# Two-block transformer on one core: the experts' part as a fixed chain of steps, with 21 weight places

## The chip, the core and the metric

The program runs on one core of a Trainium2 chip. TensorE (PE) multiplies matrices into PSUM, VectorE (DVE) and ScalarE (ACT) work element by element, GpSimd (POOL) does small side work, and SyncE (SP) issues the transfers of weights from device memory (HBM) to the on-chip memory. The metric is the device time of one execution in microseconds (us); less is better.

## What is computed

x has 256 tokens of 1024 features. A first block of two layers runs mixed attention (compressed, selected and windowed attention, gated linear attention, spatial gating) and a gated FFN of width 2816. A second block of one layer runs dilated and sliding-window attention and then a mixture of experts:

```python
g_top = argmax(hf @ w_group + b_group)            # one of 4 groups per token
ids   = 2 best of the 8 experts of that group      # weights e_w, scaled by the group's probability
for e in range(32):
    a = silu(hf @ w_e_gate[e]) * (hf @ w_e_up[e])  # 1024 -> 512
    out = out + gates[:, e:e+1] * (a @ w_e_down[e])
return rmsnorm_2(x + out, g_final)
```

hf is the normed x. All 32 experts' weights are read in fp32: three matrices of 2 MB each.

## The kernel before

All instructions of the listing are recorded through one helper, so nearly every row of the profile has its line, L257; tiles tell the parts apart. `raw`, `raw_right` and `raw_left` are places for weights, 2048 fp32 columns on 128 partitions (1 MB) each; `arena` is the main arena for temporaries, `arena_y` that of the second block's attention; `y_hi` and `y_lo` hold its outputs, `h_hi` and `h_lo` the normed input in two parts for products in fp32r, `whi` and `wlo` the same for weights.

**Weights.** `Stream` holds a list of units in the order of use. `pump` issues the next units on SP's queue into the free places, in that order, and `free` gives a place back after its last matmul. A place that was lent by the arena goes back to the arena after one use. A dense unit is split on ACT and DVE into hi and lo; experts' units are used as fp32. A pair of experts q (of 16) has 12 units: eight for gate and up (two row halves, two experts, two matrices) and four for down. The order is rows and down of each pair, except that at the end it is rows 14, rows 15, down 14, down 15. Places: seven `raw` throughout; five `raw_right` once the attention's outputs are used up in `mix2`; three `raw_left` once the output projection has finished; and three of the arena, lent once, at the start of `route`. That is 18.

**Routing.** `t_xg` transposes x, weighs it with the norm's gain and computes the logits; `route` finds group, experts and, with a triangular matmul, each token's place among the at most 32 rows (`CAP`) of an expert. `h_rows` scales x by gain and norm and splits it into `h_hi` and `h_lo`.

**Experts.** They run in four batches of eight. `t_batch` builds the one-hot matrix (token to row), gathers the rows by matmuls with it into `xe` in four steps k2 of eight products, and builds `gt`, the gated matrix for the way back, from 24 small DVE operations and eight transposes. It is a task beside the main line: `S.tick` and `S.until` let a planner with its own clock emit its steps between those of the main line. A pair's rows are 32 matmuls of 32 rows by 512 columns, four at a time on different column strips of TensorE; each fp32 matmul leaves two records in the trace. `t_act` (tanh, two DVE products, four transposes, a copy) is such a task too, and the down product of pair q-1 stands between the two row halves of pair q:

```python
if h == 0 and 1 <= q < NQ - 1:
    self.emit_down(q - 1)
```

Two pairs fill `Y`, which `emit_scatter` adds to the tokens in PSUM banks 0 to 3. `last_norm` closes with the norm and the stores. A branch (L2315) handles experts with more than 32 rows.

Of the kernel before, what the change touches and what calls it, by code (L numbers as in the profile page):

```python
# [6 lines left out]
F32 = mybir.dt.float32  # L7
# [43 lines left out]
LENT = 3  # L51
# [518 lines left out]
class Kernel:  # L570
# [992 lines left out]
    def plan2(self):  # L1563
# [31 lines left out]

        for q in range(NQ):
# [255 lines left out]
    def mix2(self):  # L1852
# [57 lines left out]
    def t_xg(self, c):  # L1910
# [6 lines left out]
        s = slice(c * 512, c * 512 + 512)  # L1917
# [22 lines left out]
        if c == 0:  # L1940
            self.xgr = yield from self.ar.new(2, D)
        else:
            self.norm_rstd(self.rstd)
        (nc.vector if c else nc.gpsimd).tensor_tensor(
            out=self.xgr[:, :, s],
            in0=self.x[:, :, s],
            in1=self.gffn[:, s].unsqueeze(1).to_broadcast([P, 2, 512]),
            op=ALU.mult,
        )

    def route(self):
# [36 lines left out]
        for tb in range(2):  # L1988
            self.h_rows(tb)
        self.ar.drop(self.xgr, self.gffn)  # L1990
# [67 lines left out]
    def overflow(self):  # L2058
# [3 lines left out]
        new = self.ar.try_new  # L2062
        ov = new((2, NE))

        w = [t.rearrange("p (k c) -> p k c", k=4) for t in self.st.slots[:2]]
        assert self.st.issued == len(self.st.units) and len(w) == 2
        xg = new((NK, T))
        a, th, at = new((2, 512)), new((512,)), new((4, T))
# [7 lines left out]
        two = (self.ps(4), self.ps(6))  # L2076
# [37 lines left out]
        self.emit_x()  # L2114
        self.ar.drop(ov, xg, a, th, at)

    def h_rows(self, tb):

        nc = self.nc
        hi = self.h_hi.rearrange("p a b -> p (a b)")[:, tb * D : tb * D + D]  # L2120
        lo = self.h_lo.rearrange("p a b -> p (a b)")[:, tb * D : tb * D + D]
        t, r = self.xgr[:, tb], self.rstd[:, tb : tb + 1]
        if tb:
            nc.scalar.activation(out=t, in_=t, func=AF.Copy, scale=r)
        else:
            nc.gpsimd.tensor_scalar(out=t, in0=t, scalar1=r, scalar2=1.0, op0=ALU.mult, op1=ALU.mult)
        nc.scalar.copy(out=hi, in_=t)
        nc.gpsimd.tensor_tensor(out=lo, in0=t, in1=hi.bitcast(F32), op=ALU.subtract)

    def t_batch(self, b):  # L2130


        nc, S = self.nc, self.side
        d = self.onehot[:, b % 2]
        e0 = b * 8
        for tb in range(2):
            nc.vector.tensor_tensor(
                out=d[:, tb].rearrange("p (e s) -> p e s", e=8),
                in0=self.place[:, tb, e0 : e0 + 8].unsqueeze(2).to_broadcast([P, 8, CAP]),
                in1=self.tab("iota").unsqueeze(1).to_broadcast([P, 8, CAP]),  # L2140
                op=ALU.is_equal,
            )
        xe = self.xe[b] = yield from self.ar.new(NK, 8 * CAP)
        hi = self.h_hi.rearrange("p a b -> p (a b)")
        lo = self.h_lo.rearrange("p a b -> p (a b)")
        for k2 in range(4):

            bk = [k2] if b == 0 else (yield from S.get(1))
            ps = self.ps(bk[0])
            for i in range(2):  # L2150
                k = k2 * 2 + i
                n = 0
                for tb in range(2):

                    c0 = tb * D + (k // 4) * 512
                    c = slice(c0 + k % 4, c0 + 512, 4)
                    for h in (hi, lo):
                        self.mm(ps[:, i * 256 : i * 256 + 256], h[:, c], d[:, tb, :], n == 0, n == 3)
                        n += 1
            if b:  # L2160
                yield
            self.evict(xe[:, k2 * 2 : k2 * 2 + 2, :].rearrange("p a b -> p (a b)"), ps)
            if b:
                S.put(bk)
            S.done.add(("xe", b, k2))
            yield
        if b == 0:
            self.gates()
        dg = yield from self.ar.new(2, 2, 3, 2 * CAP)
        for tb in range(2):  # L2170
            for pr in range(2):
                for i in range(6):
                    e = e0 + 4 * pr + i % 4
                    nc.vector.tensor_scalar(
                        out=dg[:, tb, pr, i // 2, i % 2 * CAP : i % 2 * CAP + CAP],
# [463 lines left out]
```

## Time and profile before

| | us |
|---|---|
| median of 3 runs | 1471.01 |
| lowest, highest | 1468.20, 1473.86 |
| the profiled execution | 1472.58 |
| its span in the trace | 1470.8 |
| busy in it: PE, DVE, ACT, POOL | 1294.8, 740.4, 558.8, 226.4 |
| DMA traffic | 360.75 MB, mean 245 GB/s |

The profile is of one execution. Busy shares are averages over very different stages: the two layers and the second attention take the first two thirds, the experts the last. There TensorE is reported busy for much of the time, but its records are stretched by a low clock, so the GB/s row and the waits say more than the busy row.

### The profile page before, as it was taken

What the parts mean: (1) busy time and instruction counts of PE and PEld (TensorE: products, weight loads), DVE (VectorE), ACT (ScalarE), POOL (GpSimd) and SP (SyncE); (2) the same over time, 40 slices, a digit from 0 to 9 for tenths busy, and PEclk for the clock granted to TensorE, in tenths of its full rate; (3) what the DMA queues carried; (4) which work ended last, traced back from release to release, by engine and by line L of the source; (5) the groups of instructions that cost most, each with busy time, mean ns of one, the idle gap of its engine ahead of it and who ended that gap; (6) DMA issues with size and microseconds to landing.
All of it is one profiled execution on the core that took longest, in us unless ns stands there. A gap on an engine that the chain in (4) does not pass through costs nothing. (4 is left out here: it accounts for less than half of the span.)

```text
span 1470.8 us, 22896 instructions
## 1 busy us (share of the span) xinstructions
PE 1294.8 (88%) x8791; PEld 966.9 (66%) x8791; DVE 740.4 (50%) x1573; ACT 558.8 (38%) x1167; POOL 226.4 (15%) x348
## 2 busy tenths in 40 slices
PE   8989999999999999999999999978876857776576
PEld 8767999988777899988889999853323212311111
DVE  5587778756587677755766564663021200201001
ACT  5535655555526555555555455431000100100001
POOL 2154111101154111123332210120000000000000
PEclk9999999999999999999999999988987778787778
DMA  9551565556452566566435353697999899899995
GB/s 340 190 184 45 174 200 173 186 159 218 138 168 68 159 186 189 184 193 194 140 116 172 115 173 120 214 379 298 420 421 420 363 420 420 352 420 420 420 417 242
DMA packets 153558, 360.75 MB, mean 245 GB/s; under 512 B 8640, under 2 KB 98240, under 8 KB 128736
## 3 DMA queue, kind: packets, MB, share of 16 engines
q1 hardware_dynamic: 151328, 354.81, 66.1%
q0 software_dynamic: 1328, 3.63, 0.8%
q8 instruction: 71, 1.16, 0.3%
q10 hardware_dynamic: 784, 0.76, 0.2%
q14 instruction: 47, 0.39, 0.1%
HBM read 358.12 MB, written 1.05 MB: 244 GB/s over the span
## 5 line engine op out<-in xcount | busy, mean ns | idle before, releaser
L257 DVE TENSOR_TENSOR wlo<-raw,whi 128x512 fp32r<-128x512 f32 (+3 forms) x560 | 404.9, 730 | 255.4 <-ACT whi L257 243.2
L257 ACT CAST whi<-raw 128x512 fp32r<-128x512 f32 (+3 forms) x560 | 337.7, 606 | 341.6 <-PE psum L257 271.6
L257 PE MATMUL psum<-h_hi,whi 128*128 128x256 f32 x1040 | 296.0, 285 | 3.0 <-ACT whi L257 3.0
L257 PE MATMUL psum<-h_lo,whi 128*128 128x256 f32 x1040 | 290.6, 279 | 0.1
L257 PE MATMUL psum<-h_hi,wlo 128*128 128x256 f32 x1040 | 290.6, 279 | 0.2 <-DVE wlo L257 0.2
L257 PE MATMUL psum<-raw,arena 128*32 128x512 f32 x704 | 181.7, 696 | 58.9 <-DMA raw<-in_w_e_gate_dram 47.5
L257 DVE COPY arena<-psum 128x384 f32<-128x384 f32 (+4 forms) x68 | 38.1, 560 | 346.9 <-ACT arena L257 232.7
L257 PEld LDWEIGHTS psum<-h_hi,whi 128*128 128x128 f32 x1040 | 195.8, 188 | 10.1 <-issue 4.8
L257 PEld LDWEIGHTS psum<-h_lo,whi 128*128 128x128 f32 x1040 | 195.9, 188 | 0.9 <-issue 0.5
L257 PEld LDWEIGHTS psum<-h_hi,wlo 128*128 128x128 f32 x1040 | 195.8, 188 | 0.4 <-DVE wlo L257 0.4
L257 PE MATMUL psum<-raw_right,arena 128*32 128x512 f32 x496 | 143.8, 671 | 24.7 <-DMA raw_right<-in_w_e_gate_dram 17.1
L257 PE MATMUL psum<-whi,h_hi 128*128 128x256 f32 (+3 forms) x448 | 145.7, 325 | 1.4 <-ACT arena_o L257 1.1
L257 PE MATMUL psum<-whi,h_lo 128*128 128x256 f32 (+3 forms) x448 | 138.2, 308 | 0.0
L257 PE MATMUL psum<-wlo,h_hi 128*128 128x256 f32 (+3 forms) x448 | 138.1, 308 | 0.0
L257 PEld LDWEIGHTS psum<-raw,arena 128*32 128x32 f32 x704 | 38.8, 122 | 148.7 <-DMA raw<-in_w_e_gate_dram 62.5
L257 PE MATMUL psum<-raw_left,arena 128*32 128x512 f32 x312 | 110.3, 714 | 26.3 <-DMA raw_left<-in_w_e_gate_dram 20.4
L257 PE MATMUL psum<-arena 64*128 64x256 f32 (+10 forms) x668 | 115.4, 381 | 6.7 <-DVE arena L257 4.7
L257 ACT COPY arena<-psum 128x384 f32<-128x384 f32 (+3 forms) x61 | 32.0, 524 | 221.8 <-PE psum L257 212.4
L257 ACT ACTIVATE arena<-psum 128x256 f32<-128x256 f32 (+3 forms) x38 | 18.1, 476 | 240.7 <-PE psum L257 228.6
L257 POOL TENSOR_TENSOR arena<-arena 128x512 f32<-128x512 f32 (+2 forms) x46 | 49.2, 1079 | 295.6 <-DVE arena L257 286.6
L257 PEld LDWEIGHTS psum<-whi,h_hi 128*128 128x128 f32 x448 | 85.0, 190 | 11.0 <-issue 4.4
L257 PEld LDWEIGHTS psum<-arena 64*128 64x128 f32 (+4 forms) x668 | 63.0, 178 | 42.2 <-issue 22.1
(240 smaller groups left out, 1823.9 us busy)
## 6 DMA issues: line engine op xcount, KB each, us to landing
raw<-in_w_in_dram SPq DMA_DIRECT2D x60, 512.0 KB, 4.9
raw<-in_w_e_up_dram SPq DMA_DIRECT2D x30, 1024.0 KB, 19.8
raw<-in_w_e_down_dram SPq DMA_DIRECT2D x30, 1024.0 KB, 19.9
raw<-in_w_e_gate_dram SPq DMA_DIRECT2D x28, 1024.0 KB, 19.9
raw<-in_w_gate_dram SPq DMA_DIRECT2D x44, 512.0 KB, 4.0
raw<-in_w_up_dram SPq DMA_DIRECT2D x44, 512.0 KB, 5.0
raw_right<-in_w_e_down_dram SPq DMA_DIRECT2D x22, 1024.0 KB, 19.9
raw<-in_w_down_dram SPq DMA_DIRECT2D x20, 1024.0 KB, 5.1
```

The source lines that it names most:

```text
L257: return f(*args, **kw)
```

## The change

- The one-hot gather takes x itself in fp32 (`h_rows`, `xgr` and the 0.5 MB load of the norm's gain go). The gain is applied when the product is copied to `xe`, per feature from the small tile `gp`; the norm's factor is applied per expert row in the activation (`scales`, `rhe`, `r2e`).
- `t_batch` becomes `side_batch`, a list of eight steps: `places`, four `rows`, `scales`, two `back`. `back` builds a half of the gated matrix with four DVE operations. `moe` takes the steps from a list at fixed points, one or two at a time; the planner is not asked any more.
- A pair is one chain: rows half 0, steps, rows half 1, activation with steps, transposes, down of the same pair. The order of units is rows and down for each pair, and the last down is in eight units of 0.5 MB, column half 0 ahead of half 1, each followed by its scatter, squares and product with the final gain.
- Five fp32 matmuls without use (`WARM`) stand at the start of `route`.
- Places: seven `raw`; two in `arena_y` from the end of the attention on; three `raw_right`; one kept for good in the main arena, two lent once beside it, one more lent when `mx` is done; five `raw_left`, over the space of `h_hi`, `h_lo`, `whi` and `wlo`. That is 21. The one-hot matrix also lies in `arena_y`. The main arena is 96 columns smaller.

```diff
-LENT = 3
+WARM = 5
+LENT = 2
@@ plan2
         for q in range(NQ):
             rows(q)
-            if q < NQ - 2:
-                down(q)
-        down(NQ - 2)
-        down(NQ - 1)
+            (down if q < NQ - 1 else last_down)(q)
@@ mix2
         self.open_raw("right")
-        self.gffn = self.ar.now(D)
-        nc.gpsimd.dma_start(out=self.gffn, in_=self.A["g_ffn_2"].to_broadcast([P, D]))
+        self.st.slots.append(self.room(2048))
+        self.lend(LENT)
...
                 S.until(("mx", k))
+                if c == 0 and k == NK - 1:
+                    self.ar.drop(mx)
+                    self.lend(1)
                 self.dense_T(acc, self.h_hi, self.h_lo, [k], start=k == 0, stop=k == NK - 1)
-            if c == 1:
-                self.ar.drop(mx)
-                self.open_raw("left")
@@ route
         S.until(("xg", 0), ("xg", 1))
-        S.free = [7]
-        for _ in range(LENT):
-            self.st.lend(self.ar.now(2048), self.ar.drop)
-        self.st.pump()
+
+        self.open_raw("left")
+        self.ar.drop(self.xg)
+        for _ in range(WARM):
+            self.mm(self.ps(0), self.ident, self.x[:, 0, 0:512], True, True)
...
-        for tb in range(2):
-            self.h_rows(tb)
-        self.ar.drop(self.xgr, self.gffn)
@@ new functions
+    def lend(self, n):
+
+        for _ in range(n):
+            self.st.lend(self.room(2048), self.ar.drop)
+        self.st.pump()
...
+        def rows(k2):
+            xe = self.xe[b]
+
+            ps = self.ps(7 if b else k2).rearrange("p (k c) -> p k c", k=2)
             for i in range(2):
                 k = k2 * 2 + i
                 for tb in range(2):
 
+                    c0 = (k // 4) * 512
+                    self.mm(ps[:, i, :], self.x[:, tb, c0 + k % 4 : c0 + 512 : 4], d[:, tb, :], tb == 0, tb == 1)
+            gain = lambda k: self.gp[:, k // 4, k % 4 : k % 4 + 1]
+            k = k2 * 2
+            nc.scalar.activation(out=xe[:, k, :], in_=ps[:, 0, :], func=AF.Copy, scale=gain(k))
+            nc.vector.tensor_scalar(out=xe[:, k + 1, :], in0=ps[:, 1, :], scalar1=gain(k + 1), scalar2=None, op0=ALU.mult)
...
+        steps = [places] + [lambda k2=k2: rows(k2) for k2 in range(4)] + [scales]
+        return steps, [lambda pr=pr: back(pr) for pr in range(2)]
@@ moe
+            self.emit_rows(q, 0)
+            if q == 1:
+                todo += late
...
+            side(2)
+            self.emit_rows(q, 1)
+            if q == 0:
+                side(1)
+            th = self.emit_act(q)
+            side(2)
             if q % 4 == 3:
+                side(99)
                 self.ar.drop(self.xe.pop(b))
+            at = self.emit_at(th)
+            side(1)
             if q == NQ - 1:
...
+                break
+            self.emit_down(q, at, None)
+            self.ar.drop(at)
+            if q % 2:
+                todo[:0] = [lambda quad=q // 2, c=c: self.emit_scatter(quad, c) for c in range(2)]
+            side(1)
+        self.last_norm(at)
@@ last_norm
         for c in range(2):
+            self.emit_down(NQ - 1, at, c)
+            self.emit_scatter(NQ // 2 - 1, c)
             for tb in range(2):
@@ open_raw
         if side == "right":
-            self.ar.shrink("b")
             self.close("right")
-            n = 45 // 8
+            n = 3
         else:
             self.close("split")
-            n = 3
+            self.close("h")
+            n = 5
@@ body
+        self.ar.shrink("b")
+        self.st.slots += [self.arena_y[:, i * 2048 : i * 2048 + 2048] for i in range(2)]
+        self.onehot = self.arena_y[:, 4096 : 4096 + 32 * CAP].rearrange("p (b t c) -> p b t c", b=2, t=2)
+        self.st.pump()
         self.mix2()
```

Three places show how the order of instructions changes (the helper has line L258 in the changed kernel). The first is SP's queue at the opening of the last places, each row one unit of 1 MB. Before:

```order
L257 DMA raw5_86<-in_w_e_down_2_dram 128x2048
L257 DMA raw_left0_9339<-in_w_e_gate_2_dram 128x2048
L257 DMA raw_left1_9340<-in_w_e_up_2_dram 128x2048
L257 DMA raw_left2_9341<-in_w_e_gate_2_dram 128x2048
L257 DMA arena_88<-in_w_e_up_2_dram 128x2048
L257 DMA arena_88<-in_w_e_gate_2_dram 128x2048
L257 DMA arena_88<-in_w_e_up_2_dram 128x2048
L257 DMA raw2_83<-in_w_e_gate_2_dram 128x2048
```

In the changed kernel:

```order
L258 DMA arena_86<-in_w_e_down_2_dram 128x2048 x3
L258 DMA raw3_82<-in_w_e_gate_2_dram 128x2048
L258 DMA arena_y_6387<-in_w_e_up_2_dram 128x2048
L258 DMA arena_86<-in_w_e_gate_2_dram 128x2048
L258 DMA arena_y_6387<-in_w_e_up_2_dram 128x2048
L258 DMA raw_left0_9375<-in_w_e_gate_2_dram 128x2048
L258 DMA raw_left1_9376<-in_w_e_up_2_dram 128x2048
L258 DMA raw_left2_9377<-in_w_e_gate_2_dram 128x2048
L258 DMA raw_left3_9378<-in_w_e_up_2_dram 128x2048
L258 DMA raw_left4_9379<-in_w_e_down_2_dram 128x2048
L258 DMA raw4_83<-in_w_e_down_2_dram 128x2048
```

Before, `raw_left` and after it the three arena units end the list of 18, and the last row goes to the first place that a pair has to free. Now the units in the arena and in `arena_y` come ahead of `raw_left`, whose five end the list of 21; the last row is again the first that a pair has to free.

The second is TensorE's queue from the last transposes of x to the first expert product; `s` is the one-hot selection that the ranking matmul reads. Before:

```order
L257 MATMUL psum<-tab_67,x 128x128 x8
L257 MATMUL psum<-wr,arena 128x36 x8
L257 MATMUL psum<-s_9417,tab_67 128x64
L257 MATMUL psum<-s_9417,ones 128x32
L257 MATMUL psum<-onehot,h_hi 128x256
L257 MATMUL psum<-onehot,h_lo 128x256
```

In the changed kernel:

```order
L258 MATMUL psum<-tab_67,x 128x128 x8
L258 MATMUL psum<-wr,arena 128x36 x8
L258 MATMUL psum<-x,tab_67 128x512 x5
L258 MATMUL psum<-s_9426,tab_67 128x64
L258 MATMUL psum<-s_9426,ones 128x32
L258 MATMUL psum<-arena_y,x 128x256 x8
L258 MATMUL psum<-raw_83,arena 32x512
L258 MATMUL psum<-raw_81,arena 32x512
L258 MATMUL psum<-raw_84,arena 32x512
L258 MATMUL psum<-raw_79,arena 32x512
```

Five products of x with the identity now stand ahead of the ranking matmul, and the gather reads x and `arena_y` (the one-hot matrix) in fp32 in one piece of two steps.

The third is VectorE's queue behind the branch for overfull experts, to the end of the program. Before:

```order
L257 SCALAR_TENSOR_TENSOR arena<-arena,psum 64x512
L257 TENSOR_TENSOR arena<-arena,psum 64x512
L257 COPY arena<-psum 64x512 x2
L257 TENSOR_TENSOR arena<-psum,arena 128x512 x4
L257 TENSOR_SCALAR arena<-arena,rstd 128x512 x2
```

In the changed kernel:

```order
L258 SCALAR_TENSOR_TENSOR arena<-arena,psum 64x512
L258 SCALAR_TENSOR_TENSOR arena<-arena,r2e,psum 64x512
L258 TENSOR_TENSOR arena<-psum,arena 128x512 x2
L258 COPY arena<-psum 64x512
L258 TENSOR_TENSOR arena<-psum,arena 128x512 x2
L258 TENSOR_SCALAR arena<-arena,rstd 128x512 x3
```

The two copies of `Y` and the four products with the final gain stood in two blocks; now a pair of products stands behind the work on column half 0 and ahead of the copy for half 1, and VectorE scales three of the four last tiles.

## Rows read from the trace of the kernel before

**Rows 1.** The page's forty slices of 36.8 us: granted clock and GB/s.

```profile
PEclk9999999999999999999999999988987778787778
...
GB/s 340 190 184 45 174 200 173 186 159 218 138 168 68 159 186 189 184 193 194 140 116 172 115 173 120 214 379 298 420 421 420 363 420 420 352 420 420 420 417 242
```

**Rows 2.** Stretches: from:to, length, granted clock, DMA share, GB/s.

```profile
980.00:994.00 14.00, 0.54 1.01 425
994.00:1005.00 11.00, 0.81 0.10 20
...
1005.00:1100.00 95.00, 0.87 1.01 419
...
1140.00:1155.00 15.00, 0.61 0.72 279
...
1265.00:1285.00 20.00, 0.67 0.74 294
```

**Rows 3.** SP's issues in order of time: start us, duration, queue, destination<-source.

```profile
951.14 0.33 SPq L257 DMA_DIRECT2D raw_right<-in_w_e_gate_dram  x1
...
977.79 0.33 SPq L257 DMA_DIRECT2D raw_left<-in_w_e_gate_dram  x1
...
980.34 0.42 SPq L257 DMA_DIRECT2D arena<-in_w_e_up_dram  x1
1003.38 0.33 SPq L257 DMA_DIRECT2D raw<-in_w_e_gate_dram  x1
```

**Rows 4.** SP's waits from 1005 on (us, times, longest); a page row of issues.

```profile
SPq L257 <- PE psum L257: 135.3, 36, 19.5
SPq L257 <- DMA raw<-in_w_e_up_dram: 41.0, 20, 3.8
...
raw<-in_w_e_up_dram SPq DMA_DIRECT2D x30, 1024.0 KB, 19.8
```

**Rows 5.** Timeline of the routing: start us, duration, engine, operation, count [idle before].

```profile
979.87 2.48 PE L257 MATMUL psum<-wr,arena 128*128 128x36 f32 x16 [0.35 <-DVE arena L257]
...
984.02 4.65 POOL L257 TENSOR_TENSOR h_lo<-arena,h_hi 128x1024 fp32r<-128x1024 f32 x2 [1.16 <-ACT h_hi L257]
...
984.66 1.74 DVE L257 TENSOR_TENSOR tt<-el,top8a 128x16 f32<-128x16 f32 x1
...
986.43 2.26 DVE L257 TENSOR_TENSOR tt<-tt,tab 128x16 f32<-128x16 f32 x1
...
989.55 0.17 DVE L257 TENSOR_TENSOR tt<-e,top8b 128x16 f32<-128x16 f32 x1
...
990.88 0.69 PE L257 MATMUL psum<-s,tab 128*128 128x64 f32 x2 [8.53 <-DVE s L257]
```

**Rows 6.** Timeline of the first pair on TensorE.

```profile
999.37 0.51 PE L257 MATMUL psum<-onehot,h_hi 128*128 128x256 f32 x1
...
1001.45 1.92 PE L257 MATMUL psum<-raw,arena 128*32 128x512 f32 x16
```

**Rows 7.** Timeline of the work for batch 2 of the experts, three rows.

```profile
1137.69 5.04 DVE L257 TENSOR_SCALAR arena<-tab,place,g 128x32 f32<-128x32 f32 x24
...
1143.65 0.59 ACT L257 ACTIVATE arena<-psum 64x512 f32<-64x512 f32 x1 [0.99 <-PE psum L257]
...
1147.20 3.64 PE L257 MATMUL psum<-raw_right,arena 128*32 128x512 f32 x16 [0.47 <-ACT arena L257]
```

**Rows 8.** Timeline of the end.

```profile
1435.26 1.06 PE L257 MATMUL psum<-raw_right,arena 128*32 128x512 f32 x1 [2.29 <-DMA raw_right<-in_w_e_up_dram]
...
1440.53 0.59 ACT L257 ACTIVATE arena<-psum 64x512 f32<-64x512 f32 x1 [9.70 <-PE psum L257]
...
1458.36 0.58 ACT L257 COPY arena<-psum 64x512 f32<-64x512 f32 x1 [9.56 <-PE psum L257]
...
1458.99 3.70 PE L257 MATMUL psum<-arena 128*128 128x512 f32 x8 [0.68 <-ACT arena L257]
...
1463.57 0.18 POOL L257 TENSOR_TENSOR v<-ssq 128x2 f32<-128x2 f32 x1 [136.00 <-ACT psum L257]
```

More of the change, by code (lines that the diff above doesn't have):

```diff
@@ L1939, in t_xg @@
                 yield
-        if c == 0:
-            self.xgr = yield from self.ar.new(2, D)
-        else:
+        if c:
             self.norm_rstd(self.rstd)
[L1944 to L1949, printed above, removed]
     def route(self):
@@ L2135, in t_batch @@
         e0 = b * 8
[L2136 to L2145, printed above, removed]
@@ L2146, in t_batch, with places @@
-        for k2 in range(4):
-            bk = [k2] if b == 0 else (yield from S.get(1))
-            ps = self.ps(bk[0])
+        def places():
+            for tb in range(2):
+                nc.vector.tensor_tensor(
+                    out=d[:, tb].rearrange("p (e s) -> p e s", e=8),
+                    in0=self.place[:, tb, e0 : e0 + 8].unsqueeze(2).to_broadcast([P, 8, CAP]),
+                    in1=self.tab("iota").unsqueeze(1).to_broadcast([P, 8, CAP]),
+                    op=ALU.is_equal,
+                )
+            self.xe[b] = self.room(NK, 8 * CAP)
@@ L2160, in t_batch @@
[L2160 to L2175, printed above, removed]
-                        in0=self.tab("iota"),
-                        scalar1=self.place[:, tb, e : e + 1],
-                        scalar2=self.gate[:, tb, e : e + 1],
-                        op0=ALU.is_equal,
-                        op1=ALU.mult,
-                    )
-            yield
@@ L2183, in t_batch @@
-        gt = yield from self.ar.new(2, 2, T)
-        for pr in range(2):
-            bk = yield from S.get(1)
-            ps = self.ps(bk[0])
+                    c0 = (k // 4) * 512
[4 more added lines that the diff above has]
+            nc.vector.tensor_scalar(out=xe[:, k + 1, :], in0=ps[:, 1, :], scalar1=gain(k + 1), scalar2=None, op0=ALU.mult)
@@ new lines, in scales @@
+        def scales():
+            ps = self.ps(7)[0:64, 0:4]
+            for q in range(4):
+                for tb in range(2):
+                    self.mm(ps[:, q : q + 1], d[:, tb, q * 64 : q * 64 + 64], self.rstd[:, tb : tb + 1], tb == 0, tb == 1)
+            rh, r2 = self.small([64, 4], "rhe", bufs=2), self.small([64, 4], "r2e", bufs=2)
+            nc.scalar.activation(out=rh, in_=ps, func=AF.Copy, scale=0.5)
+            nc.vector.tensor_tensor(out=r2, in0=rh, in1=rh, op=ALU.mult)
+            self.re[b] = rh, r2
@@ L2206, in t_act, with emit_act @@
+    def emit_act(self, q):
+        nc = self.nc
+        gu = self.ps(4)
+        rh, r2 = (t[:, q % 4 : q % 4 + 1] for t in self.re[q // 4])
+        th = self.room(512)
+        nc.scalar.activation(out=th[0:64], in_=gu[0:64], func=AF.Tanh, scale=rh)
         nc.vector.scalar_tensor_tensor(
@@ L2257, in emit_scatter @@
[L2257 to L2272 removed]
+                    self.st.free(units[(c or 0) * 4 + k // 2 * 2 + x])
@@ L2274, in moe @@
+        if not odd:
+            self.Y = self.room(2, 512)
+        for i in cs:
+            copy = nc.scalar.copy if i == 0 else nc.vector.tensor_copy
+            copy(out=self.Y[r[i] : r[i] + 64, i], in_=y[r[i] : r[i] + 64])
     def moe(self):
-        nc, S = self.nc, self.side
+        nc = self.nc
         self.gates = self.route()
-        self.xe, self.gt, self.at = {}, {}, {}
+        self.xe, self.gt, self.re = {}, {}, {}
         nb = NQ // 4
-        S.start(self.t_batch(0), ("batch", 0))
```

300 lines of the change are left out of this document (145 added, 155 removed).

## The prediction

> **What bounds the kernel now.** I read the page's forty slices first, then a table of stretches, then the DMA issues, the waits of the issuing queue and the end. The slices [rows 1] split the span in two. Through the first 26 TensorE holds its full clock and mostly 70 to 220 GB/s are moved; in the last twelve 420 GB/s pass at most times while the granted clock is 0.7 to 0.8. So the last 470 us are set by the experts' weights: 192 units of 1 MB (32 experts, six each, 1.0486 MB apiece). At the 419 GB/s of the long even stretch [rows 2] a unit takes 2.50 us and all of them 480 us.
>
> That stream has three holes. From 994 to 1005 it moves 20 GB/s, and in 1140:1155 and 1265:1285 it falls to 279 and 294 [rows 2]. The issues explain the first [rows 3]: the eighteenth unit is issued at 980.34, the next at 1003.38. All 18 places are full until TensorE has used the first four units. Later SP, the queue that issues them, waits now for an earlier transfer to land and now for TensorE to free a place, but a unit takes 19.8 us from issue to landing, eight times 2.50 us: eight are in flight, and only a wait for TensorE of about that length opens a hole. The longest is 19.5 [rows 4]. Whatever shortens the holes or the end shortens the run; a faster engine inside the even stretches does not.
>
> **The change, part by part.** *Places at the start.* 21 instead of 18: three more units are in before the stream runs dry, 3 x 2.50 = **7.5 us**. I checked that they can get there. Two loads of w_out_2 now go to arena_y, so six expert units rather than four are out when raw_right opens at 951.14; fifteen remain, 37.5 us, that is 988.6, and the last five must wait for raw_left, which opened at 977.79 [rows 3] and should again. The stream then runs dry near 991 instead of 994.
>
> *When it starts again.* This hangs on the first half of the first pair. (a) Routing: two VectorE operations took 1.74 and 2.26 us where a like one takes 0.17, while GpSimd ran the two h_lo subtractions (4.65 us) [rows 5]. Those subtractions are gone: 4.00 - 0.34 = 3.7 us less. (b) The five WARM products are new and stand ahead of the routing's matmul. TensorE is free from 979.87 + 2.48 = 982.35 to 990.88 [rows 5]. An fp32 product of 512 columns leaves two records of 3.70/8 = 0.46 us [rows 8], about 0.43 apart: ten make 4.3 us at full clock, 8.5 at half. They end between 986.6 and 990.9 and are wanted at 990.88 - 3.7 = 987.2; the delay is 0 to 3.7, and I take 1.0, since the clock is low there, 0.54 over 980:994 [rows 2], and a run of full products should lift it midway. (c) Before, a one-hot step of 2.1 us stands between the two quarters of the first half (999.37 to 1001.45) [rows 6]; now both steps that the half needs stand ahead of it and none in between: 2.1 less. (d) The step is now fp32 from x, four products, eight records. No row shows it; half of 0.43 is 0.21 per record, so 1.7 us, against 2.1 now; at half clock 3.4. Two steps: -0.8 to +2.7, I take +0.3. Together 3.7 - 1.0 + 2.1 - 0.3 = **4.5 us** earlier (0 to 6).
>
> *The two later holes.* A batch's work lies in one lump: from the one-hot products through 24 VectorE operations (5.04 us) and the transposes, no weights are freed for some 20 us (the 19.5 above), and only at 1147.20 the held down product runs [rows 7]. Afterwards it is eight steps, at most two at a time between half pairs, with four larger VectorE operations per half batch in place of twelve. Eighteen lasting places less eight in flight leave ten units, 25 us of cover, against two steps of about 2.1 + 0.85 us. I let both holes go: 15 x (1 - 279/419) + 20 x (1 - 294/419) = 5.0 + 6.0 = **11.0 us**.
>
> *The pair as one chain.* The activation of a pair no longer runs beside the next pair's rows: TensorE does rows, transposes, down in order. At full clock two k take 1.92 us at 1001.45 [rows 6], so eight for the rows take 7.7 and four for the down 3.8; the activation chain 3.5 (1143.65 to 1147.20 [rows 7]); scatter, steps and their copies some 5: 20 us. The stream needs 12 x 2.50 = 30. Cost nothing, hidden by the transfers; if that cover is gone, see the second rival.
>
> *The end.* Before, both last pairs' rows came ahead of both downs; the last row unit (number 184) landed at 1435.26 and the span ended 35.5 us later [rows 8]. Now it is number 188, 4 x 2.50 = 10.0 us later in the stream, and after it TensorE has a chain to run: rest of the rows 5.3 (1435.26 to 1440.53); activation to down 3.5; down of half 0: four k on two column strips, not four, so as long as a whole down, 3.8 at full and 7.3 at half clock (3.64 for two k [rows 7]), I take 5.0; copy and scatter 0.7 + 1.85; down of half 1 3.5; copy, the last two scatters and squares 3.4 (1458.36 to 1463.57 is 5.2, less half of 3.70); GpSimd to the end 6.8 (7.2 less an estimated 0.4, since ACT scales one tile before its stores, not two) [rows 8]. Sum 30.0 (28.5 to 35). Against the 35.5: 10.0 + 30.0 - 35.5 = **+4.5 us**. Half 1's weights land 10 us after the last row unit and are wanted at 16, so cutting four units into eight halves costs nothing. The Trainium skill (DMA: Bandwidth & Descriptors, Anatomy of one DMA and Bandwidth) speaks against it: a transfer costs about 2.0 us plus bytes/436e3, and its rule is batches of 1 MiB or more. By that the cut would add 8 us of fixed cost and the end would be some 2 us later (an estimate from that page); with eight in flight the rows show units landing 2.50 us apart, so the fixed part is covered here.
>
> *Small things.* The final gain (0.5 MB) is now fetched among the last units: +0.5 us. The gain of the ffn norm in 0.5 MB goes, but that transfer lay ahead of the first hole: 0. Row scales (eight tiny products a batch) and the gains in the copies lie under the transfers: 0. The main arena is 96 columns smaller, and the planner places some steps of the two attention layers otherwise (two places of the order, near 80 to 130 and 415 to 470 us); the same instructions, so 0, with 3 us either way.
>
> **Sum.** -7.5 - 4.5 - 11.0 + 4.5 + 0.5 = -18.0 us. The profiled execution took 1472.58 (span 1470.8), so 1454.6; the median of the runs shown is 1471.01, 1.6 below it, so the forecast is **1453 us**.
>
> **The rivals.** *Half clock where it counts.* WARM late, first steps and both last downs at half clock: the restart gains 0.5 instead of 4.5 and the end takes 35 instead of 30: 1453 + 4 + 5 = 1462. For it: a granted 0.7 to 0.8 [rows 1] is half clock for some 40% of the stage; against: a run of matmuls has lifted it each time.
>
> *TensorE becomes the bound, and the run is slower.* At half clock rows 14.6, down 7.3, the rest as the parts above doubled where they are matmuls: about 34 us a pair, over the 30 of the stream. Four more us in each of fifteen pairs is +60: 1513. It decides when the share of half clock passes 0.71 (20 + 14 x share = 30), and the run is slower than before past 0.80. For it: each pair now has bare waits inside. Against: a TensorE that lags has no transfers to wait for, and the long matmul runs of [rows 6] went at full speed. The Trainium skill (TensorE: Matmul & The Clock Gate, HAM oscillation) describes just this, work after every DMA wait starting cold. By that rule taken whole the pairs would stay at 34; the trace agrees in part, at 0.7 to 0.8 granted.
>
> *The holes stay.* If the lumps were not what held the stream, 11 us come back: 1464. Against: no weight is freed in them.
>
> *The places come late*, the change doing less than it says: SP issues in order, and a load into the arena or arena_y that must wait for a reader holds everything behind it. Held from 956 to the opening of raw_left at 978, the stream loses 12 us: 1465.
>
> *More than that*: no delay by WARM, the end at full clock throughout, the layers 3 us better: 1446.
>
> **How the numbers follow.** Forecast (1448 to 1459) 0.55; half clock 0.15; holes stay 0.10; late places 0.05; TensorE bound 0.05; more 0.10. The range from 1445 to 1465 leaves out the slower tail and a little at the bottom. A measurement here can tell about 0.5%, 7.4 us, from no change, so faster means under 1463.6. That holds for the forecast, half clock, the better case and part of the hole case: 0.84; same 0.10; slower 0.06.
>
> **What would show it.** Right: the DMA row has 420 GB/s from about 1001 to 1420 without the two holes; 21 units are issued before the stream's first stop, and that stop ends near 1000; the VectorE operations of routing are all 0.2 us; the last row unit lands near 1421 and 30 us follow. Wrong: idle DMA next to SP waits for PE in the even part (places or TensorE short), a low clock with TensorE busy without waits for DMA (TensorE bound), the issues after raw_right opens held back, or more than 35 us after the last row unit.

## The result, and the profile after

The changed kernel takes 1452.82 us, the median of 4 runs (1452.72 to 1454.15), against 1471.47 for the kernel before (1468.2 to 1473.86): a ratio of 0.9877, 95% interval 0.9857 to 0.9897. Its profiled execution took 1452.91 with a span of 1451.1, 19.7 us less than the 1470.8 of before.

The page's forty slices of the changed kernel, of 36.3 us each, granted clock and GB/s, beside [rows 1]:

```profile
PEclk9998999999999999999999999999989979988888
...
GB/s 342 193 170 47 162 179 199 167 195 177 178 96 147 131 189 183 186 188 225 152 94 169 117 163 141 220 327 354 419 420 420 421 421 420 420 421 421 421 419 211
```

From the 29th slice on the GB/s row is flat; the two slices of 363 and 352 are gone. The same stretches as in [rows 2] (from:to, length, granted clock, DMA share, GB/s):

```profile
980.00:994.00 14.00, 0.88 1.01 422
994.00:1005.00 11.00, 1.00 0.52 191
1005.00:1100.00 95.00, 0.91 1.01 421
1140.00:1155.00 15.00, 1.00 1.01 421
1265.00:1285.00 20.00, 0.85 1.01 421
```

The first stop now lies between about 996 and 1001, and TensorE has its full clock there. SP's issues that answer [rows 3], in order of time, and its waits for TensorE from 1005 on (us, times, longest), which answer [rows 4]:

```profile
955.03 0.33 SPq L258 DMA_DIRECT2D raw_right<-in_w_e_gate_dram  x1
...
981.40 0.33 SPq L258 DMA_DIRECT2D raw_left<-in_w_e_gate_dram  x1
...
983.19 0.43 SPq L258 DMA_DIRECT2D raw_left<-in_w_e_down_dram  x1
1000.59 1.28 SPq L258 DMA_DIRECT2D raw<-in_w_e_down_dram  x3
```

```profile
SPq L258 <- PE psum L258: 31.6, 19, 6.6
```

Unit 21 is issued at 983.19 and unit 22, the first into a freed place, at 1000.59; before, unit 18 at 980.34 and unit 19 at 1003.38. Both raw_right and raw_left open later than before, by 3.9 and 3.6 us. From 1005 on SP waits 31.6 us for TensorE, not 135.3, and never over 6.6 at a time. Routing and the first pair (start, duration, engine, operation, count), beside [rows 5] and [rows 6]:

```profile
985.52 6.23 PE L258 MATMUL psum<-x,tab 128*128 128x512 f32 x10
985.79 0.42 DVE L258 SCALAR_TENSOR_TENSOR lg<-psum,rstd,br 128x36 f32<-128x36 f32 x2 [1.53 <-issue]
...
990.28 0.22 DVE L258 TENSOR_TENSOR s<-oh4a,sel 128x64 f32<-128x64 f32 x1
...
991.59 0.33 PE L258 MATMUL psum<-s,tab 128*128 128x64 f32 x2
...
992.90 4.11 PE L258 MATMUL psum<-arena_y,x 128*128 128x256 f32 x16 [0.78 <-DVE arena_y L258]
...
996.94 3.64 PE L258 MATMUL psum<-raw,arena 128*32 128x512 f32 x32
```

No VectorE operation between the logits and `s` is longer than 0.42 us. The five idle products (x10, 6.23 us) hold the ranking product, wanted at 990.5, until 991.59. The end, beside [rows 8]:

```profile
1421.40 3.62 PE L258 MATMUL psum<-raw,arena 128*32 128x512 f32 x26 [1.46 <-DMA raw<-in_w_e_up_dram]
...
1425.06 0.68 ACT L258 ACTIVATE arena<-psum,rhe 64x512 f32<-64x512 f32 x1 [20.49 <-PE psum L258]
...
1428.57 0.62 PE L258 MATMUL psum<-raw,arena 128*32 128x512 f32 x1 [0.53 <-ACT arena L258]
...
1433.94 0.58 ACT L258 COPY arena<-psum 64x512 f32<-64x512 f32 x1 [5.42 <-PE psum L258]
...
1440.17 0.68 DVE L258 COPY arena<-psum 64x512 f32<-64x512 f32 x1 [2.10 <-PE psum L258]
...
1443.76 0.18 POOL L258 TENSOR_TENSOR v<-ssq 128x2 f32<-128x2 f32 x1 [24.99 <-ACT psum L258]
```

The last row unit lands at 1421.40, and 29.7 us follow to the end of the span.

### The profile page after: what moved, and what is told of

The parts are those of the page before. It is cut to its first block, busy times and chain, and to the rows that moved or that the text cites. A ratio compares the mean times of both kernels' runs of the same rounds, so it can differ in the third digit from the quotient of the medians.

```text
span 1451.1 us, 23004 instructions
## 1 busy us (share of the span) xinstructions
PE 1311.3 (90%) x8865; PEld 977.9 (67%) x8865; DVE 724.6 (50%) x1521; ACT 559.8 (39%) x1175; POOL 215.9 (15%) x345
## 4 chain that ended last, share of the span: by engine, by line
PE 41%; DMA 22%; DVE 3%; ACT 2%; POOL 1%; issue 1%; POOLq 0%; DVEq 0%; SPq 0%; ACTq 0%
PE psum L258 41%; DMA raw<-in_w_e_up_dram 8%; DMA raw_left<-in_w_e_down_dram 3%; DMA arena_y<-in_w_e_up_dram 3%; DMA raw<-in_w_e_down_dram 3%; DMA raw_right<-in_w_e_up_dram 3%; DMA raw_right<-in_w_e_down_dram 1%; DMA raw_left<-in_w_e_up_dram 1%; DVE arena L258 1%; ACT whi L258 1%; ACT arena L258 1%; DVE wlo L258 1%; POOL arena L258 1%; DVE arena_o L258 0%; ACT arena_o L258 0%
## 5 line engine op out<-in xcount | busy, mean ns | idle before, releaser
L258 DVE TENSOR_TENSOR wlo<-raw,whi 128x512 fp32r<-128x512 f32 (+3 forms) x552 | 397.2, 727 | 260.5 <-ACT whi L258 249.4
L258 ACT CAST whi<-raw 128x512 fp32r<-128x512 f32 (+3 forms) x552 | 332.8, 606 | 344.6 <-PE psum L258 274.4
L258 PE MATMUL psum<-h_hi,whi 128*128 128x256 f32 x1040 | 297.8, 286 | 3.0 <-ACT whi L258 3.0
L258 PE MATMUL psum<-h_lo,whi 128*128 128x256 f32 x1040 | 291.6, 280 | 0.1
L258 PE MATMUL psum<-h_hi,wlo 128*128 128x256 f32 x1040 | 290.2, 279 | 0.0
L258 PEld LDWEIGHTS psum<-h_hi,whi 128*128 128x128 f32 x1040 | 195.8, 188 | 10.1 <-issue 4.8
L258 PEld LDWEIGHTS psum<-h_lo,whi 128*128 128x128 f32 x1040 | 196.2, 189 | 0.9 <-issue 0.5
L258 PEld LDWEIGHTS psum<-h_hi,wlo 128*128 128x128 f32 x1040 | 196.0, 188 | 0.2 <-DVE wlo L258 0.2
L258 PE MATMUL psum<-raw,arena 128*32 128x512 f32 x608 | 164.0, 672 | 19.1 <-DMA raw<-in_w_e_up_dram 12.6
L258 PE MATMUL psum<-arena 64*128 64x128 f32 (+10 forms) x752 | 160.1, 418 | 21.6 <-DVE arena L258 8.2
L258 PE MATMUL psum<-whi,h_hi 128*128 128x256 f32 (+3 forms) x448 | 145.8, 325 | 1.4 <-ACT arena_o L258 1.1
L258 PE MATMUL psum<-whi,h_lo 128*128 128x256 f32 (+3 forms) x448 | 138.3, 309 | 0.0
L258 PE MATMUL psum<-wlo,h_hi 128*128 128x256 f32 (+3 forms) x448 | 138.3, 309 | 0.0
L258 PEld LDWEIGHTS psum<-arena 64*128 64x128 f32 (+4 forms) x752 | 73.1, 175 | 69.8 <-issue 23.7
L258 DVE SCALAR_TENSOR_TENSOR arena<-arena,psum 128x256 f32<-128x256 f32 (+2 forms) x36 | 17.8, 517 | 201.7 <-ACT arena L258 198.8
L258 PEld LDWEIGHTS psum<-raw,arena 128*32 128x32 f32 x608 | 34.4, 121 | 99.8 <-issue 60.3
L258 PE MATMUL psum<-raw_left,arena 128*32 128x512 f32 x400 | 81.2, 712 | 20.9 <-DMA raw_left<-in_w_e_gate_dram 14.8
L258 POOL TENSOR_TENSOR arena<-arena 128x512 f32<-128x512 f32 (+2 forms) x46 | 49.0, 1074 | 295.3 <-DVE arena L258 289.0
L258 PEld LDWEIGHTS psum<-whi,h_hi 128*128 128x128 f32 x448 | 85.3, 190 | 11.0 <-issue 4.4
L258 PEld LDWEIGHTS psum<-wlo,h_hi 128*128 128x128 f32 x448 | 85.4, 191 | 4.6 <-issue 1.4
L258 PEld LDWEIGHTS psum<-whi,h_lo 128*128 128x128 f32 x448 | 85.2, 190 | 4.5 <-DVE h_lo L258 0.2
L258 DVE COPY arena<-psum 128x384 f32<-128x384 f32 (+6 forms) x60 | 32.6, 543 | 108.0 <-ACT arena L258 95.7
```

What stands on the lines that cost most here:

```text
L258: return f(*args, **kw)
```

## The experiments

Each is the changed kernel with an edit, unless it says otherwise. A ratio is against the kernel before on the same chip, whose median there was 1468.4 to 1469.7; beside the changed kernel it was 1471.5. So a difference in us between two runs carries some 2 to 3 us of that.

**Three places fewer.** The two slots of arena_y and the place lent when mx is done are left out.

```diff
-                    self.lend(1)
-        self.st.slots += [self.arena_y[:, i * 2048 : i * 2048 + 2048] for i in range(2)]
```

> The changed kernel without three of its 21 places: the two in arena_y and the one lent when mx is done. Theory (each place more at the first stop is one unit, 2.50 us, earlier in the stream, and the later holes went because the batch's work is spread): 18 issues before the first stop, 7.5 us later, no later hole, 1452.8 + 7.5 = 1460. Rival (it was the lasting places, of which this one has 16 and before had 15, that closed the holes at 1140 and 1265): both holes come back too, 1460 + 11 = 1471. Second rival (the places only fill while the stream is dry anyway): 1453.

1460.37 us (ratio 0.9934, 0.9917 to 0.9950), 7.6 more than the changed kernel (8.4 by the ratios), with no hole behind 1005. The theory holds: three places are worth three units at the first stop and nothing later. The 16 lasting places alone bring no hole back.

**The batch in one lump**, with all 21 places:

```diff
                 todo += sum(self.side_batch(b + 1), [])
+                side(99)
```

> The changed kernel with all 21 places, but the eight steps of each later batch emitted in one lump ahead of a pair, as before did. Theory (the lump holds the release of weights for some 17 to 20 us, and 18 lasting places less eight in flight cover 25): no hole, or one of under 2 us, 1453 to 1455. Rival (the lump by itself makes the holes, whatever the places): about 5 us at each of the three batches that come later, the GB/s row falls to 350 to 370 there, 1463 to 1468.

1462.65 us (0.9959, 0.9937 to 0.9981), 9.8 more than the changed kernel (12 by the ratios). The number is near the rival's, the mechanism nobody's: not three holes of 5 us but one of 11.7, added up from stretches of 2.5 us, at the first lump. SP's issues there, then three stretches (length, clock, DMA share, GB/s):

```profile
1037.29 0.38 SPq L258 DMA_DIRECT2D raw<-in_w_e_up_dram  x1
1064.57 0.33 SPq L258 DMA_DIRECT2D raw<-in_w_e_gate_dram  x1
```

```profile
1057.50:1065.00 7.50, 0.64 0.00 0
1140.00:1155.00 15.00, 0.73 1.01 421
1265.00:1285.00 20.00, 0.91 1.01 421
```

SP issues nothing for 26.9 us; eight transfers in flight last until 1055. At the second lump the same pause is 4.4 us. A reading that fits: places stand free only after TensorE, some 20 us a pair by the prediction's own count against 30 of the stream, has gained on the stream for several pairs; at 1040, two pairs behind the stop, it has not. In the changed kernel SP's pauses of more than 4 us all end by 1042. So where the steps stand matters most right behind the first stop.

The kernel before had no such hole. Its planner spread the first later batch between the rows, and SP paused twice, 9.7 and 9.6 us, ahead of these issues:

```profile
1069.47 0.33 SPq L257 DMA_DIRECT2D raw_right<-in_w_e_down_dram  x1
...
1080.82 0.33 SPq L257 DMA_DIRECT2D raw<-in_w_e_up_dram  x1
```

So for this batch the run is no way back to the kernel before; it is for the second and third, which stood in one lump there.

**Both at once.**

> Both edits of the two runs before it at once: three places fewer (16 lasting, 18 at the start) and each later batch in one lump. Apart they cost 7.5 and 9.8 us. Theory A (the lump only hurts while no place stands free, that is right after the first stop; two places fewer change nothing later on): the costs add, 1452.8 + 7.5 + 9.8 = 1470, one hole near 1055 to 1065 and none later. Theory B (the lump and the number of lasting places together made the holes of before at 1140 and 1265): holes at the later batches too, 5 us each, 1480.

1468.8 us (0.9993, 0.9978 to 1.0008): the costs nearly add, 16.0 us of 17.4, as theory A said, with one hole of 6.5 us near 1060 and none later; SP's pause at the two later lumps is 6.0 and 5.9 us. So the lump and the places, apart or together, are not enough to make the holes at 1140 and 1265.

**The held down product too.** In addition to both edits a pair's down product waits for the next pair's rows, much as before had it (the test for overflow has to move behind the last rows). It is not quite the order of before: there the down product stood between the two halves of the next pair's rows, and the lump behind the first half; here it waits for both halves, and the lump stands ahead of the first.

```diff
             self.emit_rows(q, 1)
+            if held is not None:
+                self.emit_down(q - 1, held, None)
...
-            self.emit_down(q, at, None)
+            held = at
```

> The changed kernel with three of the changes undone together: 18 places at the start, each later batch in one lump, and the down product of a pair held back until the next pair's rows are done, as before had it; the test for overflow stands behind the last rows. Places and lump together gave 1468.8 and no hole behind 1100 us. Theory (the holes of before at 1140 and 1265 need the held down product: its four units stay in their places beside the next pair's, so fewer places stand free when the lump comes): holes of 4 us or more at each of the two later batches, and 1476 to 1482. Rival (holding it back costs nothing, because the places that stand free cover it): no hole behind 1100, 1466 to 1470.

1482.31 us (1.0080, 1.0051 to 1.0108). No hole behind 1100, so the theory as written failed, and its time came about otherwise. The hole at the first later batch grew from 6.5 to about 13 us, and from the landing of the last row unit to the end of the span it is 40.6 us, not 29.7: the down product of pair 14 now stands there, and TensorE is idle 6.23 us behind the test for overflow and the activation. But SP's pauses at the later lumps grew from 6 to 15.9 and 14.3 us, just under what eight transfers in flight cover.

**One lasting place fewer still**, 15 as before had.

```diff
-            n = 5
+            n = 4
```

> The run before it with one more lasting place taken away, the fifth of raw_left: 15 lasting places as in the kernel before, 17 at the start. There the stream's issues paused 15.9 us at the second later batch and 14.3 at the third, and no hole followed, since eight transfers in flight last 17.5 to 20 us; the kernel before paused 20.2 at both. Theory (the free places are what is left of the lasting places beside eight in flight and the held down units; one fewer lengthens each pause by 2.5 us or by a whole half pair, past what is in flight): pauses of 18 us or more and a hole of 1 to 5 us at each, 1485 to 1495. Rival (the pauses of the kernel before are its own longer batch, 24 VectorE operations and the transposes): pauses of 14 to 17, no hole behind 1100, 1482 to 1485, the 2.5 us of the first stop alone.

1487.1 us (1.0131, 1.0105 to 1.0156), and smaller holes are back at the two batches. Two stretches, first of the run before this one, then of this one:

```profile
1142.50:1147.50 5.00, 0.69 1.02 419
1265.00:1270.00 5.00, 0.99 1.00 411
```

```profile
1142.50:1147.50 5.00, 0.84 0.65 221
1265.00:1270.00 5.00, 1.00 0.91 341
```

SP's pauses are 18.6 and 16.5 us; the holes, added up from stretches of 2.5 us, 2.5 and 1.1 us. Of the pauses one is as the theory asked and one short of it. The whole ladder:

| kernel | lasting places | pauses at the second and third later batch, us | holes there, us |
|---|---|---|---|
| changed | 18 | under 4 | 0 |
| lump | 18 | 4.4, under 4 | 0 |
| lump | 16 | 6.0, 5.9 | 0 |
| lump, held down | 16 | 15.9, 14.3 | 0 |
| lump, held down | 15 | 18.6, 16.5 | 2.5, 1.1 |
| before | 15 | 20.2, 20.2 | 5.0, 6.0 |

The largest step is the held down product, though it was tried only on top of the lump with 16 places, and held half a pair longer than before had it. So the ladder shows that lump, held product and few places together make holes at these batches; whether spreading the steps alone would have closed them, with the product still held, was not tried. From the last rung but one to the kernel before some 2 to 4 us of pause are left; its batch is longer (24 VectorE operations, 5.04 us [rows 7]) and stands otherwise, but that was not tried by itself.

**Without the idle products** (WARM 5 to 0):

> The changed kernel without the five idle products ahead of routing, which compute nothing that is used. Theory (they hold the ranking product 1.0 us but keep the gather at full clock): without them the ranking starts 1.0 us earlier, the two gather steps and the first row units run at half clock, 4.1 to 8 us for the steps, so the first freed place comes 3 to 5 us later and the time rises to 1456 to 1458. Rival (the gather's own run lifts the clock within a few us, as long runs did before): 0 to 1 us faster, 1452 to 1453.

1453.98 us (0.9897, 0.9878 to 0.9916), not to be told from the changed kernel. Two stretches of this run, then of the changed kernel:

```profile
985.00:991.00 6.00, 0.50 1.02 425
991.00:997.00 6.00, 0.71 0.63 259
```

```profile
985.00:991.00 6.00, 0.72 1.01 422
991.00:997.00 6.00, 1.00 0.89 365
```

The clock stays at 1.2 GHz until the gather itself has lifted it: its first half takes 5.48 us, not 4.11, while the ranking starts at once.

```profile
991.13 5.48 PE L258 MATMUL psum<-arena_y,x 128*128 128x256 f32 x16 [0.78 <-DVE arena_y L258]
```

From the opening of raw_left to the first freed place it is 20.1 us, against 19.2. Between these two executions the idle products give back 0.9 us, less than the theory's 3 to 5 and more than the rival's nothing. But that is within what one execution differs from the next. Over the ten profiled executions with the idle products (the changed kernel and the runs made from it) the same stretch takes 18.3 to 20.2 us. In three of them the gather takes 5.6 us, as if the idle products were not there; one is the run of the next experiment:

```profile
984.67 4.54 PE L258 MATMUL psum<-x,tab 128*128 128x512 f32 x10
...
991.49 5.62 PE L258 MATMUL psum<-arena_y,x 128*128 128x256 f32 x16 [0.85 <-DVE arena_y L258]
```

There the idle products ran at full clock (4.54 us, granted 1.00) and delayed nothing, and the granted clock fell to 0.62 and 0.53 in the first four us of the gather. So a gain by the idle products is not shown.

**A GpSimd subtraction beside routing.**

```diff
+        nc.gpsimd.tensor_tensor(
+            out=self.arena_y[:, 4096:5120], in0=self.x[:, 0], in1=self.x[:, 1], op=ALU.subtract
+        )
```

> The changed kernel with one GpSimd subtraction more, 128x1024 of two SBUF tiles, set beside the VectorE operations of routing; its result is not used. Theory (the VectorE operations of 1.7 and 2.3 us in the kernel before were held by the GpSimd subtraction beside them, 4.65 us long): one to three VectorE operations of routing become 1.5 us or longer, the ranking product starts 1 to 3.5 us later, and since the stream stands still there the whole run is that much longer, 1454 to 1456. Rival (what held them was the copies of ScalarE, or their own data): every VectorE operation stays at 0.2 us and the time at 1452.8.

1452.59 us (0.9881, 0.9862 to 0.9899): the price is the rival's, the mechanism the theory's. The timeline of this run:

```profile
983.69 2.34 POOL L258 TENSOR_TENSOR arena_y<-x 128x1024 f32<-128x1024 f32 x1
...
985.39 0.16 DVE L258 TENSOR_REDUCE top4a<-lg 128x2 f32<-128x8 f32 x1
985.58 0.47 DVE L258 TENSOR_TENSOR tt<-lg,top4a 128x8 f32<-128x8 f32 x1
```

The subtraction ends at 986.03. The reduction with one input goes through beside it; the VectorE operation with two inputs from SBUF ends at 986.05, 0.30 us late. In [rows 5] the row of GpSimd is two subtractions, 4.65 us together, so they end near 986.35 and 988.67; the two slow VectorE operations end at 986.40 and 988.69. In a second profile of the kernel before the same two take 2.14 and 2.26 us. So the 3.7 us of before were waits for the end of a GpSimd operation; how much one costs depends on where the next operation with two inputs falls. The Trainium skill (SBUF — State Buffer, Who interferes with whom) says that a DVE instruction with two SBUF inputs contends with a GpSimd instruction that reads SBUF, and that a reduction never does. The three rows agree.

**The last two pairs' rows first**, as before had it, with the halves of the last down product kept.

```diff
+            if q < NQ - 2:
+                down(q)
+        down(NQ - 2)
+        last_down(NQ - 1)
```

> The changed kernel with the last two pairs in the order of before: rows of pair 14, rows of pair 15, then down 14, then the eight half units of down 15. The same bytes. Theory (the end is what TensorE still has to do once the last byte has landed, and after the change that is 19.7 us: half an activation chain, both halves of the down product, scatter, norm): now only the last part of half 1 is left behind the last byte, 1.5 + 3.6 + 7.3 = 12.4 us, so the span ends 7 us earlier, 1445 to 1447. Rival (TensorE, at half clock between waits, takes as long as the 10 us that the four units of down 14 need): 1452.8.

1450.76 us (0.9874, 0.9855 to 0.9892): 2 us below the changed kernel, with intervals that overlap almost wholly, so no change is shown. The last byte lands at about 1431.4 and 17.0 us follow, not 12.4; in the changed kernel it is 1432.8 and 18.3. TensorE in this run:

```profile
1406.59 2.48 PE L258 MATMUL psum<-raw_left,arena 128*32 128x512 f32 x3 [2.78 <-PEq L2341]
1412.27 1.06 PE L258 MATMUL psum<-raw_left,arena 128*32 128x512 f32 x2 [3.21 <-issue]
...
1421.23 4.89 PE L258 MATMUL psum<-raw,arena 128*32 128x512 f32 x32
...
1427.56 0.62 PE L258 MATMUL psum<-raw,arena 128*32 128x512 f32 x1 [1.44 <-DVE arena L258]
```

The last rows start behind the test for overflow (L2341) and an idle stretch that the profile puts to no wait, run at half clock, and from there activation, both down products and scatter follow in one chain, with no wait for a transfer. The rival was near: TensorE, not the stream, ends this order.

**Three pairs' rows first**, with the test moved behind the last activation.

> The changed kernel with the rows of the last three pairs ahead of their three down products, the test for overflow moved behind the last activation, the same bytes. In the run with two pairs so ordered TensorE, not the transfers, still set the end: rows of pair 15 began 1.9 us after their last unit landed, behind the test for overflow, and ran at half clock, 5.8 us. Theory (with one more pair ahead, TensorE waits for each unit of the last down product, and behind the last byte lie 8 products, copy, scatter, squares, 1 + 0.7 + 2 + 1.3, and 7.3 to the end): the span ends 12.5 us after the last byte, as against 16.5 with two pairs and 18.5 in the changed kernel: 1446 to 1448. Rival (the wait for each unit lowers the clock, and the last half down, scatter and copy double): 3 us later, 1449 to 1451.

1460.16 us (0.9927, 0.9903 to 0.9951), worse than both said. TensorE there:

```profile
1411.92 0.71 PE L258 MATMUL psum<-tab,arena 64*128 64x64 f32 x4 [2.36 <-DVE arena L258]
1418.31 1.93 PE L258 MATMUL psum<-raw_left,arena 128*32 128x512 f32 x6 [5.68 <-ACTq L2364]
1423.76 1.93 PE L258 MATMUL psum<-raw_left,arena 128*32 128x512 f32 x8 [3.52 <-issue]
```

The test (L2364) and what follows it cost TensorE 9.2 us, and all three down products still lie ahead. Neither theory had priced the test; where it stood it had cost 0.5 us.

**The layers' 4 us.** The kernel before with the smaller arena, then the changed kernel with the old one, then the kernel before once more.

```diff
-        N_RAW, N_SPLIT, ARENA = 7, 6, 12032
+        N_RAW, N_SPLIT, ARENA = 7, 6, 11936
```

> The kernel before with one number changed: the main arena 96 columns smaller, as the change has it. Theory (the smaller arena alone makes the two attention layers end later, as the first issue into raw_right at 955.0 us against 951.1 shows): the first issue into raw_right moves to 954.5 to 955.5, and the time rises by 3.5 to 4, from 1471.5 to about 1475. Rival (the 4 us come from something else in the change, or from one execution to the next): the issue stays at 951 and the time at 1471.5.

> The changed kernel with the main arena at its old 12,032 columns and nothing else altered, so that the layers' instructions come in the order of before. Theory: the first issue into raw_right comes at 951 again, everything behind it moves up, and the time falls by 3.5 to 4, from 1452.8 to about 1449. Rival (the layers' order is not the cause, or the supply of weights absorbs it, because the transfers and not the layers set the start): 1452.8 and an issue at 955.

> The kernel before, unchanged, for a second profile of it. Theory (the layers' 4 us are the smaller arena's): the first issue into raw_right again at 951 us, within 1. Rival (the layers of one and the same program differ by some us from execution to execution, as the spread of its times, 1464 to 1477, makes likely): elsewhere, 3 us or more away.

The first gave 1476.18 us (1.0038, 1.0016 to 1.0061), slower by about 6, the second 1452.17 (0.9873, 0.9853 to 0.9893), no change, the third 1470.95 in one run. The first issue into raw_right, in this order:

```profile
957.50 0.33 SPq L257 DMA_DIRECT2D raw_right<-in_w_e_gate_dram  x1
```

```profile
955.99 0.33 SPq L258 DMA_DIRECT2D raw_right<-in_w_e_gate_dram  x1
```

```profile
951.87 0.33 SPq L257 DMA_DIRECT2D raw_right<-in_w_e_gate_dram  x1
```

Two executions of the kernel before are 0.7 us apart. But the changed kernel and the nine runs made from it at this arena size, whose layers have the same instructions in the same order on every engine, made this issue between 953.20 and 956.58 us; the latest is that of the run with three pairs' rows first:

```profile
956.58 0.33 SPq L258 DMA_DIRECT2D raw_right<-in_w_e_gate_dram  x1
```

One execution can thus differ from the next by 3 us, and the rival of chance is not excluded. The smaller arena makes the kernel before slower over six runs; the 6.4 us in its layers rest on one execution. The old arena, which gives the changed kernel the layers' old order on every engine, does not take the delay away in the execution profiled (1454.1, at the upper end of its 1449.0 to 1454.4). How much of the 4 us is order, chance or something else stays open; where the tiles lie in SBUF still differs and was not tried.

## Why the prediction came out as it did

The forecast was 1453 us, the result 1452.8. That agreement is better than its steps, and partly luck: errors of +3.6 in one term and of -1.9 and -2.6 in two others nearly cancel. The span's 19.7 us, taken apart in the trace of the changed kernel:

| step | forecast, us | measured, us |
|---|---|---|
| layers | 0 (3 either way) | +3.6 (raw_left opens at 981.40, not 977.79) |
| three places more | -7.5 | -7.5 (21 units out, not 18, counted at 2.50 us; 7.6 by the run without them) |
| restart, from the opening of raw_left | -4.5 | -6.4 (19.2 to the first freed place, not 25.6) |
| later holes | -11.0 | -13.6 |
| end | +4.5 | +4.2 (10.0 + 29.7 - 35.5) |
| final gain | +0.5 | not seen apart |
| sum | -18.0 | -19.7 |

*The layers* are the mis-sized term that would have mattered: "the same instructions, so 0" was wrong by 3.6 us in the execution profiled, more than the 3 it was given (1.8 to 5.2 over the ten executions with these layers), and the cause is open. What hid it are two terms that were too small.

*The places* were right in size and kind. The stream of the kernel before also stood nearly still for some 3 us ahead of the opening of raw_left (184 and 98 GB/s in 975:977.5 and 977.5:980), which the prediction did not list; it cost nothing, since all 18 units were in before the first place came free.

*The restart.* The collision was worth 3.67 us (8.38 from the logits to `s` before, 4.71 after), the delay by the idle products 1.04; both as forecast. The rest gave 3.8 where parts (c) and (d) together gave 1.8: 2.1 for the step that no longer stands between the quarters, as (c) has it; 0 for (d), the two steps taking 4.04 us to the first row product as against 4.05, where 0.3 more was forecast; and 1.7 that no part had, 0.8 in the row products of the first half, 0.6 from the ranking to the gather and 0.3 ahead of the logits. The ranking and the first pair now run at a granted 1.00, where the kernel before had 0.54 until 994 and 0.81 to 1005 [rows 2]; the forecast counted nothing for that. At full clock two steps take 4.11 us, 0.26 per record and not 0.21. The 6.4 lies just outside the 0 to 6 that the part was given, and the ten executions with the idle products would give 5.4 to 7.3, by the clock (18.3 to 20.2 us in place of 19.2).

*The holes.* From the first freed place to the landing of the last row unit the kernel before took 431.9 us for 166 units, the changed one 420.8 for 167; at 2.52 a unit the difference is 13.6. The two holes are 11.0 of it, as in the sum; part of the rest is the rate, 421 GB/s against 419. The size was right, the reason was incomplete. "The lumps" do not explain the holes by themselves: a lump alone makes no hole at these two places. With the down product held beside the next pair and 15 lasting places it does, and the step that the prediction priced at nothing, the pair as one chain, is the largest rung of the ladder (6 us of pause against 15). Putting the steps in lumps costs 9.8 us by itself, but at another place, right behind the first stop, where the kernel before had spread them; it is no part of the gain.

*The end.* Last row unit at 1421.40 (forecast 1421), then 29.7 us (30.0): rows 3.7 (5.3), activation 3.5 (3.5), down of half 0 5.4 (5.0), its copy and scatter 2.6 (2.55), down of half 1 3.7 (3.5), copy, scatter and squares 3.6 (3.4), to the end 7.3 (6.8). The granted clock in half 0 is 0.50 for its second part, as the forecast allowed for. The last byte lands at 1432.8 and half 1 begins at 1436.50 without a wait for it, so cutting the last units into halves cost nothing, as forecast.

*The rivals.* Half clock did not reach the restart in the execution profiled; in three of the ten with the idle products it took part of the gather, 1.5 us. The better case adds up to 1447.5 by its own terms (1.0, 1.5 and 3 us), not 1446. TensorE did not become the bound: SP waits little for it. The holes did not stay, and the places came in time: the stream moves 416 to 426 GB/s from 965 to 995.

## What to carry to other kernels

In a stream of weights count three things: places, transfers in flight, and the longest time in which nothing is released. A pause of the issues shows in the time only once it outlasts what is in flight (in the two runs with the product held, 15.9 us left no hole and 16.5 one of 1.1), so read the pauses on the issuing queue and not the holes alone: they tell how near a kernel stands to one. Side work is cheap where free places have built up and dear right after a stop; and a product held back keeps its places with it.

## What the runs showed of the hardware

- A test of a value with a branch on all engines cost TensorE 0.5 us where it waits for transfers anyway, and 9.2 us (5.68 of wait and 3.52 that the profile puts to issue) where its operands were there; in the run with two pairs it was 2.78 of wait and 3.21 of issue. The Trainium skill (Runtime: NRT & Kernel Launch, Instruction fetch mechanics) says that a taken branch to code outside the window held forces a fetch before execution goes on. That would fit the part put to issue; no run here shows the fetch itself.
- VectorE operations with two inputs from SBUF end within 0.05 us of the end of a GpSimd operation that runs beside them, three times of three in the rows shown.
- Ten executions of programs whose layers have the same instructions in the same order on every engine reached the same point between 953.20 and 956.58 us. It is not explained; a difference of 3 us between two single profiles shows nothing by itself.
- Five idle products did not settle the clock of the gather behind them: over ten executions it took 4.11 us seven times and 5.6 three times.
